# Encoder layer on one core: single-column float32 products in the matmul stream, filter loads moved, first transfers regrouped

## The chip, the cores and the metric

The kernel is one program on one core of a Trainium2 chip. Times are device microseconds (us) of that core. TensorE does the matmuls (PE in the rows; PEld are its weight loads), VectorE (DVE) and ScalarE (ACT) do the elementwise work, GpSimd (POOL) almost nothing, and SyncE (SP) issues most DMA transfers. The engines run side by side and wait for each other by semaphores.

## The reference

The input is x, 256 tokens by 2048 channels, float32. What is computed, cut to its shape:

```
h = rmsnorm(x, norm_mix);  p = h @ w_in            # 2048 -> 4352 columns, shared by three mixers
y_a = pooling over 2/4/8/16 tokens, per-group linear         (512 channels)
y_b = x0 * (conv(x1*v) + d*x1*v), width-3 convolved inputs; conv is a 256-long two-sided
      filter made by a small sine network (two sine layers)  (768 channels)
y_c = u * (128x128 token mixing of layernorm(v)), u, v = gelu (768 channels)
x = x + concat(y_a, y_b, y_c) @ w_out              # 2048 x 2048
h = rmsnorm(x, norm_ffn)
up = dwconv3(h @ ffn_w_up)                         # 2048 -> 11264
x = x + (silu(gate) * val) @ ffn_w_down            # 5632 -> 2048
out = rmsnorm(x, norm_final)
```

## The kernel before

All weights are float32 and are read once from HBM. Every operand of a large product is split into a rounded part (hi) and a rest (lo), and a product is three float32r products: hi with hi, hi with lo, lo with hi. `load_split` (L92) issues the transfer of a chunk on SP, makes hi on ACT (L105) and lo on DVE (L106). Chunks are kept in rings: four raw buffers, three hi and three lo.

The stages, in order of time:

- **v product** (L217, to 42 us): tokens on the partitions, 16 steps over the 2048 input channels, each with 12 products of 384 columns (L233 to L235). Step k needs a 128x768 chunk of weights and a 128x256 piece of x, scaled by the first norm's weight `gmix` (L196, `load_x`). Beside it run the squares for the norm, and the two sine layers that make the filters (`filter_layer1`, L267, and `filter_layer2`, L280: one small float32 product each, L273 and L282, seven DVE operations, one sine on ACT).
- **w_in tiles** (to 226 us): 28 tiles of 128 output channels. A tile is 16 pairs of products (`chunk_products`, L130): one of 512 columns (L137, weights hi, activations hi and lo side by side) and one of 256 (L138, weights lo). Between the chunks of a tile `tick` runs what `at` has put into a slot: the filter's spectrum (`taps_load`, `taps`, `filter_spectrum`), transposes (L408), the forward and inverse transforms (L126 to L128, L459 and L460), pooling (L512) and token mixing (L554). These are the interruptions of the stream of pairs.
- **w_out** (226 to 316 us, 256 pairs on `yT`), **w_up** (to 806 us, 88 tiles, 1408 pairs on `actB`), **w_down** (to 989 us, 528 pairs on `gT`). Shortly after w_up begins come the sums of squares (`sum_cols`, L162: two float32 products of one column) and the broadcast of the norm (`rms_rows`, L180).
- **the last 512 output channels** (L725, `products`), with tokens on the partitions and 512 columns a product, and `finish` (L694): square and sum on ACT, the root, DVE's scaling, the transfers out.

The order on each engine is made by a scheduler from priorities. Loads stand ahead by `tc.high_priority(offset=AHEAD)`. Each engine then works strictly in that order.

A float32 product (not float32r) runs as two records in the trace; so "x4" in a row of L162 is two products.

Of the kernel before, what the change touches and what calls it, by code (L numbers as in the profile page):

```python
# [11 lines left out]
F32 = mybir.dt.float32  # L12
# [25 lines left out]
NWARM = 8  # L38
NAUX = 2

C_GFFN, C_GFIN = 0, 16
# [11 lines left out]
def encoder_layer(ctx, tc, a):  # L53
# [15 lines left out]

    big.tile([P, 24], F32, name="pad_big")  # L70
    xT = big.tile([P, KT, L], F32, tag="xT", name="xT")
    gmix = const.tile([P, KT], F32, name="gmix")
    with tc.high_priority(offset=1000):
        nc.scalar.dma_start(gmix, a["gmix"])
    par = const.tile([P, C_N], F32, name="par")
# [15 lines left out]

    def load_split(src, n, pieces=1, into=None, raw=None, between=None):  # L92
        with tc.high_priority(offset=AHEAD):
            if raw is None:
                raw = wp.tile([P, CW], F32, tag="raw", name="raw", bufs=4)
            hi, lo = into or (wp.tile([P, CW], F32R, tag=t, name=t) for t in ("hi", "lo"))
            for i in range(pieces):
                s = slice(i * n // pieces, (i + 1) * n // pieces)
                (nc.scalar if between and i == 0 else nc.sync).dma_start(raw[:, s], src[:, s])
# [16 lines left out]
    def tick():  # L116
        clock[0] += 1
        for f in slots.pop(clock[0] - 1, []):
            f()

    def split(hi, lo, src):
# [74 lines left out]
    def load_x(ks):  # L196
        nc.sync.dma_start(xT[:, ks[0]:ks[-1] + 1, :], a["xT"][:, ks[0]:ks[-1] + 1, :])
        for k in ks:
# [15 lines left out]
    vtok = p1.tile([P, 2, D_GM], F32, name="vtok")  # L214


    def v_product(then):  # L217
        pv = [[psm.tile([P, 512], F32, tag="mm", name="mm") for _ in range(2)] for _ in range(2)]
        p1.tile([P, 24], F32, name="pad_y")
        head = p1.tile([P, KT // 2, D_GM], F32, tag="yT", name="head")  # L220
        for k in range(KT):
            first = (lambda: load_x(x_steps[0])) if k == 0 else None
            hi, lo = load_split(a["w_v"][k], D_GM, 2 if k == 0 else 1, raw=head[:, k, :] if k < KT // 2 else None,
                                between=first)
            if k + 1 < len(x_steps):
                with tc.high_priority(offset=AHEAD):
                    load_x(x_steps[k + 1])
            for g in range(2):
# [335 lines left out]
    def filters(q, n):  # L564
        taps_load(q)
        for i in range(2):
            at(n + i, lambda i=i: taps(i))
            at(n + 2 + i, lambda i=i: filter_spectrum(q, i))
# [10 lines left out]
    for i in range(2):  # L579
        load_dft(Fh[i].rearrange("p a b -> p (a b)"), a["Fm"][i])  # L580
    filters(0, 2)
    pool_group(0)
# [9 lines left out]
    hyena_out(0, z, Ys)  # L592
    at(0, lambda: filters(1, 1))
    z, zT = hyena_z(1)
# [30 lines left out]
    for c in range(2):  # L625
        for m in range(2):
            chunk_products(head[m], w_out(m), yT, c, KT)
    for m in range(KT):
        ps, sb = (head[m], second_half(head[m])) if m < 2 else proj_tile(w_out(m), yT, KT)
# [11 lines left out]
    p2 = ctx.enter_context(tc.tile_pool(name="p2", bufs=1))  # L641
    p2.tile([P, 32], F32, name="pad_g")
    gT = p2.tile([P, NFF, 2, L], F32R, name="gT")
# [10 lines left out]
    for j in range(NFF):  # L654
        o = []
        for part in range(2):
            m = 2 * j + part
            ps, sb = up[m] if j == 0 else up_tile(m)
            nc.vector.tensor_add(sb, ps[:, :L], sb)
            s = tmp("ev")  # L660
# [33 lines left out]
    def finish(h, ps):  # L694
        t = slice(h * P, (h + 1) * P)
        wide = wp.tile([P, CW], F32, tag="raw", name="raw", bufs=4)
        sq, xt = wide[:, :NL], wide[:, NL:]
        ssq, v, s_, y, w, r = (tmp(f"fin{i}", 1) for i in range(6))
# [25 lines left out]

    def products(h, c, last):  # L725
        hi, lo = chunks[c]
        for i in range(NKC):
# [4 lines left out]
            nc.tensor.matmul(acc[h], lh, lo[:, s], start=False, stop=False)  # L732
            nc.tensor.matmul(acc[h], ll, hi[:, s], start=False, stop=last and i == NKC - 1)  # L733

    for c in range(NC):
        if c >= NKEEP:
            chunks[c] = load_split(a["w_last"][c], CW)
        products(0, c, c == NC - 1)
        if c >= NKEEP:
            products(1, c, False)  # L740
        if c == NKEEP:
            pc = sum_cols(acc3)
            nc.vector.tensor_scalar(rest, pc[:, 0:2], 1.0 / D, EPS_RMS, op0=ALU.mult, op1=ALU.add)
    for c in range(NKEEP):
        products(1, c, c == NKEEP - 1)
        if c == 1:
            finish(0, acc[0])
# [138 lines left out]
```

## Time and profile before

| | us |
|---|---|
| median of 3 runs (1061.39 to 1061.55) | 1061.5 |
| the profiled execution, its own time | 1061.44 |
| its span, first to last instruction | 1059.6 |
| PE busy | 1048.1 (99%) |
| PEld busy | 921.5 (87%) |
| DVE busy | 788.6 (74%) |
| ACT busy | 577.5 (54%) |
| DMA, mean rate | 191 GB/s |

The profiled execution is 0.06 us below the median, and 1.8 us lie around its span. PE's granted clock is half up to 5.4 us from the span's start and full from there to the end of the products. Matmuls overlap in the records (a 512-column product is shown with 391 ns though the next one starts 230 ns later), so their pace is read from start to start and not from their durations.

### The profile page before, as it was taken

How to read it: one execution, taken by the hardware profiler on the slowest of the kernel's cores; microseconds unless marked ns; L12 is line 12 of the kernel's file. 1: busy time of each engine (PE TensorE's matmuls, PEld its weight loads, DVE VectorE, ACT ScalarE, POOL GpSimd, SP SyncE). 2: the span in 40 equal slices, each digit the busy share in tenths (PEclk: the TensorE clock that was granted, in tenths of full speed). 3: DMA queues.
4: the chain of work that ended last, by engine and by line, in shares of the span. 5: the costliest groups of instructions: out<-in, count | busy, mean ns of one | idle time of the engine just before them, and what ended most of it. 6: DMA issues, size and time to landing. Idle time of an engine off the chain costs nothing.

```text
span 1059.6 us, 15714 instructions
## 1 busy us (share of the span) xinstructions
PE 1048.1 (99%) x5956; PEld 921.5 (87%) x5956; DVE 788.6 (74%) x1239; ACT 577.5 (54%) x871; POOL 1.3 (0%) x14
## 2 busy tenths in 40 slices
PE   9999999999999999999999999999999999999997
PEld 8888888888888888888888888888888888888885
DVE  6898998987767878878788888788886555565344
ACT  7765555555556555555555555555555444554332
POOL 0000000000000000000000000000000000000000
PEclk9999999999999999999999999999999999999999
DMA  8866545566555665656556665566565665676462
GB/s 289 270 193 214 173 150 172 206 193 190 187 183 190 194 191 189 194 186 195 183 196 186 191 191 188 192 187 196 184 194 176 196 188 188 229 214 206 143 192 79
DMA packets 62019, 202.83 MB, mean 191 GB/s; under 512 B 7063, under 2 KB 11896, under 8 KB 61816
## 3 DMA queue, kind: packets, MB, share of 16 engines
q1 hardware_dynamic: 61656, 201.64, 59.2%
q8 instruction: 46, 0.75, 0.3%
q10 hardware_dynamic: 288, 0.20, 0.1%
q14 instruction: 29, 0.24, 0.1%
HBM read 199.72 MB, written 2.10 MB: 190 GB/s over the span
## 4 chain that ended last, share of the span: by engine, by line
PE 98%; DVE 1%; DMA 0%; ACT 0%; issue 0%; SPq 0%; DVEq 0%; ACTq 0%
PE mm L137 56%; PE mm L138 29%; PE mm L731 2%; PE mm L733 2%; PE mm L732 2%; PE mm L234 1%; PE mm L233 1%; PE mm L235 1%; PE aux L137 1%; PE aux L127 0%; PE aux L128 0%; DMA xT<-in_xT 0%; DVE lo L106 0%; PE aux L138 0%; PE aux L126 0%; PE aux L459 0%
## 5 line engine op out<-in xcount | busy, mean ns | idle before, releaser
L105 ACT CAST hi<-raw 128x1024 fp32r<-128x1024 f32 (+1 forms) x362 | 373.9, 1033 | 432.5 <-PE mm L137 211.9
L106 DVE TENSOR_TENSOR lo<-raw,hi 128x1024 fp32r<-128x1024 f32 (+1 forms) x362 | 434.8, 1202 | 230.1 <-ACT hi L105 229.3
L137 PE MATMUL mm<-actB,hi 128*128 128x512 f32 x1408 | 488.8, 391 | 0.0
L138 PE MATMUL mm<-actB,lo 128*128 128x256 f32 x1408 | 394.2, 280 | 0.0
L137 PEld LDWEIGHTS mm<-actB,hi 128*128 128x128 f32 x1408 | 263.3, 187 | 58.0 <-DVE actB L635 0.2
L138 PEld LDWEIGHTS mm<-actB,lo 128*128 128x128 f32 x1408 | 266.1, 189 | 0.0
L137 PE MATMUL mm<-gT,hi 128*128 128x512 f32 x528 | 183.1, 391 | 0.0
L137 PE MATMUL mm<-actA,hi 128*128 128x512 f32 x416 | 148.1, 398 | 0.0
L138 PE MATMUL mm<-gT,lo 128*128 128x256 f32 x528 | 147.8, 280 | 0.0
L137 PEld LDWEIGHTS mm<-gT,hi 128*128 128x128 f32 x528 | 98.7, 187 | 21.6
L138 PE MATMUL mm<-actA,lo 128*128 128x256 f32 x416 | 116.6, 280 | 0.0
L138 PEld LDWEIGHTS mm<-gT,lo 128*128 128x128 f32 x528 | 99.8, 189 | 0.0
L137 PEld LDWEIGHTS mm<-actA,hi 128*128 128x128 f32 x416 | 78.1, 188 | 17.3
L137 PE MATMUL mm<-yT,hi 128*128 128x512 f32 x256 | 90.5, 399 | 0.0
L138 PEld LDWEIGHTS mm<-actA,lo 128*128 128x128 f32 x416 | 78.5, 189 | 0.1
L138 PE MATMUL mm<-yT,lo 128*128 128x256 f32 x256 | 71.9, 281 | 0.0
L378 ACT ACTIVATE o<-ev,par 128x256 f32<-128x256 f32 x106 | 63.3, 598 | 8.0 <-DVE ev L373 6.6
L137 PEld LDWEIGHTS mm<-yT,hi 128*128 128x128 f32 x256 | 48.1, 188 | 11.9
L380 DVE SCALAR_TENSOR_TENSOR o<-ev,par,o 128x255 f32<-128x255 f32 x106 | 51.2, 483 | 3.3
L145 ACT COPY sb<-mm 128x256 f32<-128x256 f32 x142 | 51.9, 366 | 0.0
L379 DVE SCALAR_TENSOR_TENSOR o<-ev,par,o 128x255 f32<-128x255 f32 x106 | 50.7, 479 | 0.4 <-ACT o L378 0.4
L138 PEld LDWEIGHTS mm<-yT,lo 128*128 128x128 f32 x256 | 48.4, 189 | 0.0
(208 smaller groups left out, 809.6 us busy)
## 6 DMA issues: line engine op xcount, KB each, us to landing
raw<-in_w_up SPq DMA_DIRECT2D x176, 512.0 KB, 3.5
raw<-in_w_down SPq DMA_DIRECT2D x60, 512.0 KB, 3.7
raw<-in_w_in SPq DMA_DIRECT2D x56, 512.0 KB, 3.5
raw<-in_w_out SPq DMA_DIRECT2D x32, 512.0 KB, 3.5
raw<-in_w_last SPq DMA_DIRECT2D x22, 512.0 KB, 3.5
raw<-in_w_v SPq DMA_DIRECT2D x8, 384.0 KB, 3.5
raw<-in_w_down SPq DMA_DIRECT2D x12, 256.0 KB, 2.6
head<-in_w_v SPq DMA_DIRECT2D x7, 384.0 KB, 6.4
```

The source lines that it names most:

```text
L105: nc.scalar.copy(hi[:, s], raw[:, s])
L106: nc.vector.tensor_sub(lo[:, s], raw[:, s], hi[:, s].bitcast(F32))
L137: nc.tensor.matmul(ps, hi[:, s], act[:, k, :, :], start=k == 0, stop=False)
L138: nc.tensor.matmul(ps[:, :L], lo[:, s], act[:, k, 0, :], start=False, stop=k == nk - 1)
L145: nc.scalar.copy(sb, ps[:, L:])
L233: nc.tensor.matmul(o, actA[:, k, 0, t], hi[:, s], start=k == 0, stop=False)
L378: nc.scalar.activation(o, s, AF.Identity, bias=col(b), scale=col(w1))
L379: nc.vector.scalar_tensor_tensor(o[:, 1:], s[:, :L - 1], col(w0), o[:, 1:], op0=ALU.mult, op1=ALU.add)
L380: nc.vector.scalar_tensor_tensor(o[:, :L - 1], s[:, 1:], col(w2), o[:, :L - 1], op0=ALU.mult, op1=ALU.add)
L731: nc.tensor.matmul(acc[h], lh, hi[:, s], start=False, stop=False)
L732: nc.tensor.matmul(acc[h], lh, lo[:, s], start=False, stop=False)
L733: nc.tensor.matmul(acc[h], ll, hi[:, s], start=False, stop=last and i == NKC - 1)
```

## The change

Five things are changed.

- **Single-column products.** `settle` issues one float32 product of `ones` with one column of `ones` into a spare PSUM bank and keeps it in program order. It is called after the first chunk of w_out, after w_out's first four chunks, and after tile 2 of w_up.
- **Filter loads.** The weights and the decay of the filter taps (`taps_load`), and the transform matrices `Fm`, are loaded inside slots of the w_in tiles instead of ahead of them, and each filter step comes one slot later.
- **First transfers.** `gmix` and the first piece of x come in one transfer on SP. The first chunk of v weights comes in two halves on ACT's queue into a buffer of its own. For the first three steps (`first_loads`) the order on SP, ACT and DVE is the written one.
- **The end.** The last chunk of each token half is done in two halves of 256 columns (12 products instead of 6), and `finish` squares and sums the two halves apart.
- Pads of buffers are changed so that the new buffers fit.

```
+    def settle():
+        tc.keep_in_program_order(nc.tensor.matmul(aux()[:, 0:1], ones, ones[:, 0:1], start=True, stop=True))
...
+    xg = big.tile([P, GX + KT * L], F32, tag="xT", name="xg")
+    xT = xg[:, GX:].rearrange("p (k l) -> p k l", k=KT)
+    gmix = xg[:, GX - KT:GX]
+    w_first = const.tile([P, D_GM], F32, name="w_first")
+    with tc.high_priority(offset=2000):
+        nc.sync.dma_start(xg[:, GX - KT:GX + L], a["first"])
+        nc.scalar.dma_start(w_first[:, :HC], a["w_v"][0][:, :HC])
+    with tc.high_priority(offset=1900):
+        nc.scalar.dma_start(w_first[:, HC:], a["w_v"][0][:, HC:])
...
+    def first_loads(head):
+        parts = []
+        for k in range(NFIRST):
+            if k == 0:
+                parts.append(load_split(None, D_GM, 2, raw=w_first, between=lambda: load_x(x_steps[0])))
+            else:
+                with tc.high_priority(offset=AHEAD):
+                    load_x(x_steps[k])
+                parts.append(load_split(a["w_v"][k], D_GM, raw=head[:, k, :]))
+        return parts
...
     def filters(q, n):
-        taps_load(q)
+        at(0, lambda: taps_load(q))
...
-        load_dft(Fh[i].rearrange("p a b -> p (a b)"), a["Fm"][i])
-    filters(0, 2)
+        at(2, lambda i=i: load_dft(Fh[i].rearrange("p a b -> p (a b)"), a["Fm"][i]))
+    filters(0, 3)
...
             chunk_products(head[m], w_out(m), yT, c, KT)
+            if c == m == 0:
+                settle()
+    settle()
...
             ps, sb = up[m] if j == 0 else up_tile(m)
+            if m == 2:
+                settle()
...
-        nc.scalar.activation(sq, ps, AF.Square, accum_out=ssq)
-        nc.scalar.activation(s_, ssq, AF.Sqrt, scale=1.0 / D, bias=rest[:, h:h + 1])
-        nc.vector.tensor_scalar(v, ssq, 1.0 / D, rest[:, h:h + 1], op0=ALU.mult, op1=ALU.add)
+        nc.scalar.activation(sq[:, :L], ps[:, :L], AF.Square, accum_out=sa)
+        nc.vector.tensor_scalar(more, sa, 1.0 / D, rest[:, h:h + 1], op0=ALU.mult, op1=ALU.add)
+        nc.scalar.activation(sq[:, L:], ps[:, L:], AF.Square, accum_out=ssq)
+        nc.scalar.activation(s_, ssq, AF.Sqrt, scale=1.0 / D, bias=more)
+        nc.vector.tensor_scalar(v, ssq, 1.0 / D, more, op0=ALU.mult, op1=ALU.add)
...
+    def last_products(h, c):
+        hi, lo = chunks[c]
+        for g in range(2):
+            o = acc[h][:, g * L:(g + 1) * L]
+            for i in range(NKC):
+                k = NKC * c + i
+                s = slice(i * NL + g * L, i * NL + (g + 1) * L)
+                lh, ll = (gT[:, k, j, h * P:(h + 1) * P] for j in range(2))
+                nc.tensor.matmul(o, lh, hi[:, s], start=False, stop=False)
+                nc.tensor.matmul(o, lh, lo[:, s], start=False, stop=False)
+                nc.tensor.matmul(o, ll, hi[:, s], start=False, stop=g == 1 and i == NKC - 1)
```

DVE at the program's start, before: the two halves of the first weight chunk (`head`) and the first pieces of activations (`actA`).

```order
L101 CAST hi<-head 128x384
L201 SCALAR_TENSOR_TENSOR actA<-xT,gmix,actA 128x256
L106 TENSOR_TENSOR lo<-head,hi 128x384
L201 SCALAR_TENSOR_TENSOR actA<-xT,gmix,actA 128x256
L101 CAST hi<-head 128x384
L201 SCALAR_TENSOR_TENSOR actA<-xT,gmix,actA 128x256
L106 TENSOR_TENSOR lo<-head,hi 128x384
L106 TENSOR_TENSOR lo<-head,hi 128x768
```

The same place in the changed kernel, where the first chunk is `w_first`.

```order
L111 CAST hi<-w_first 128x384
L216 SCALAR_TENSOR_TENSOR actA<-xg,actA 128x256
L116 TENSOR_TENSOR lo<-w_first,hi 128x384
L111 CAST hi<-w_first 128x384
L116 TENSOR_TENSOR lo<-w_first,hi 128x384
L216 SCALAR_TENSOR_TENSOR actA<-xg,actA 128x256
L116 TENSOR_TENSOR lo<-head,hi 128x768
```

Both halves of the first chunk now come before the second piece of activations; before, two pieces of activations stood between them.

ACT where the v product ends and the w_in tiles begin, before: the last chunk of v weights is the 768 wide CAST, the first chunks of w_in are the 1024 wide ones.

```order
L105 CAST hi<-raw 128x768
L185 ACT_TABLE_LOAD
L185 ACTIVATE rs_s<-rms_v 128x2
L294 CAST F_109<-raw 128x512
L257 ACT_TABLE_LOAD
L257 ACTIVATE w_348<-w_351 64x256
L241 ACT_TABLE_LOAD
L241 ACTIVATE vtok<-mm,rstd_mix 128x384
L105 CAST hi<-raw 128x1024 x3
```

The same place in the changed kernel.

```order
L115 CAST hi<-raw 128x768
L115 CAST hi<-raw 128x1024
L287 ACT_TABLE_LOAD
L287 ACTIVATE w_350<-w_353 64x256
L199 ACT_TABLE_LOAD
L199 ACTIVATE rs_s<-rms_v 128x2
L115 CAST hi<-raw 128x1024 x2
L271 ACT_TABLE_LOAD
L271 ACTIVATE vtok<-mm,rstd_mix 128x384 x3
```

The first chunk of w_in is now cast before the three table loads and their functions, the next two before the gelu (L271), and the cast of `Fm` (F) is gone from here.

On PE nothing of the pairs is moved. The three added products (L133) stand behind 8 pairs of w_out, 24 pairs further on, and 16 pairs behind the broadcast of the norm in w_up, where 1360 pairs on `actB` and 528 on `gT` follow without a break, as in the order before.

ACT at the end, with the semaphores that each instruction waits for, before: the root's argument and the squares of both token halves.

```order
L699 ACTIVATE raw,fin_10374<-mm 128x512 [waits PE_49]
L700 ACT_TABLE_LOAD
L700 ACTIVATE fin_10376<-fin_10374,rest 128x1 [waits Activation_49]
L699 ACTIVATE raw,fin_10414<-mm 128x512 [waits DVE_49,PE_49]
L700 ACTIVATE fin_10416<-fin_10414,rest 128x1 [waits Activation_49]
```

The same in the changed kernel.

```order
L734 ACTIVATE raw,fin_10394<-mm 128x256 [waits PE_49]
L736 ACTIVATE raw,fin_10388<-mm 128x256
L737 ACT_TABLE_LOAD [waits DVE_49]
L737 ACTIVATE fin_10390<-fin_10388,fin_10395 128x1 [waits Activation_49]
L734 ACTIVATE raw,fin_10444<-mm 128x256 [waits PE_49]
L736 ACTIVATE raw,fin_10438<-mm 128x256
L737 ACTIVATE fin_10440<-fin_10438,fin_10445 128x1 [waits DVE_49,Activation_49]
```

There are now two squares for each half of the tokens; the first waits for PE, the second has no wait for PE of its own. The count that the first waits for is the one that PE reaches with the last product of both column halves, since the twelve products raise PE's semaphore only once, at their end.

## Rows read from the trace of the kernel before

**Rows 1.** The page's chain that ended last, by engine.

```profile
PE 98%; DVE 1%; DMA 0%; ACT 0%; issue 0%; SPq 0%; DVEq 0%; ACTq 0%
```

**Rows 2.** Line L137's answer: durations ns min/median/max, first and last start in us.

```profile
L137 PE MATMUL mm<-gT,hi x528: 391/391/391, 805.8 to 988.5; 128*128 128x512 f32 x176
L137 PE MATMUL mm<-actA,hi x416: 388/395/578, 58.0 to 224.8; 128*128 128x512 f32 x139
L137 PE MATMUL mm<-yT,hi x256: 395/398/447, 226.0 to 316.2; 128*128 128x512 f32 x128
```

**Rows 3.** Timeline of PE at w_up's start: start us, us, instruction.

```profile
316.54 0.40 PE L137 MATMUL mm<-actB,hi 128*128 128x512 f32 x1
...
321.84 0.40 PE L137 MATMUL mm<-actB,hi 128*128 128x512 f32 x1
...
322.72 0.50 PE L162 MATMUL aux<-ones,acc 128*128 128x1 f32 x4
323.09 0.48 PE L137 MATMUL mm<-actB,hi 128*128 128x512 f32 x1
...
323.52 0.40 PE L137 MATMUL mm<-actB,hi 128*128 128x512 f32 x1
...
328.03 0.39 PE L137 MATMUL mm<-actB,hi 128*128 128x512 f32 x1
```

**Rows 4.** Timeline of PE around a transpose among the w_in tiles.

```profile
165.86 0.40 PE L137 MATMUL mm<-actA,hi 128*128 128x512 f32 x1
...
176.26 0.40 PE L137 MATMUL mm<-actA,hi 128*128 128x512 f32 x1
...
176.61 0.39 PE L408 MATMUL aux<-ident,z 128*128 128x128 f32 x2
...
177.20 0.40 PE L137 MATMUL mm<-actA,hi 128*128 128x512 f32 x1
...
184.97 0.40 PE L137 MATMUL mm<-actA,hi 128*128 128x512 f32 x1
```

**Rows 5.** Timeline of the first 9 us; in brackets the idle time before.

```profile
0.73 0.40 ACTq L74 DMA_DIRECT2D gmix<-in_gmix  x1
...
4.38 0.36 DVE L101 CAST hi<-head 128x384 fp32r<-128x384 f32 x1 [3.38 <-DMA head<-in_w_v]
...
5.17 0.72 PE L233 MATMUL mm<-hi,actA 128*128 128x384 f32 x2 [0.34 <-DVE actA L201]
...
7.00 0.48 DVE L201 SCALAR_TENSOR_TENSOR actA<-xT,gmix,actA 128x256 fp32r<-128x256 f32 x1 [0.73 <-ACT actA L200]
7.39 0.83 ACT L105 CAST hi<-head 128x768 fp32r<-128x768 f32 x1 [0.42 <-DMA head<-in_w_v]
7.40 0.55 DVE L106 TENSOR_TENSOR lo<-head,hi 128x384 fp32r<-128x384 f32 x1
...
8.01 0.44 PE L234 MATMUL mm<-lo,actA 128*128 128x384 f32 x1 [1.00 <-DVE lo L106]
```

**Rows 6.** Timeline of PE, then of ACT, where w_in begins.

```profile
42.07 0.34 PE L235 MATMUL mm<-hi,actA 128*128 128x384 f32 x1
43.12 0.50 PE L137 MATMUL aux<-actA,hi 128*128 128x512 f32 x1 [0.71 <-ACT hi L105]
43.46 0.59 PE L180 MATMUL aux<-rms_dg,ones 128*128 128x256 f32 x2
44.75 0.39 PE L138 MATMUL aux<-actA,lo 128*128 128x256 f32 x1 [0.69 <-DVE lo L106]
...
42.04 2.93 ACT L105 CAST hi<-raw 128x1024 fp32r<-128x1024 f32 x3
```

**Rows 7.** Timeline of ACT at the end, and the squares of 256 columns (L617).

```profile
1051.51 0.60 ACT L699 ACTIVATE raw<-mm 128x512 f32<-128x512 f32 x1 [4.78 <-PE mm L733]
1052.23 0.29 ACT L700 ACTIVATE fin<-fin,rest 128x1 f32<-128x1 f32 x1
...
L617 ACT ACTIVATE sq<-xT x26: 401/404/419, 241.7 to 992.1; 128x256 f32<-128x256 f32 x26
```

More of the change, by code (lines that the diff above doesn't have):

```diff
@@ L39 @@
 NAUX = 2
+NFIRST = 3
+GX = 64
 C_GFFN, C_GFIN = 0, 16
@@ L67, in aux @@
         return psa.tile([P, 512], F32, tag="aux", name="aux")
[L70 to L74, printed above, removed]
+    big.tile([P, 40], F32, name="pad_big")
+    xg = big.tile([P, GX + KT * L], F32, tag="xT", name="xg")
[7 more added lines that the diff above has]
+        nc.scalar.dma_start(w_first[:, HC:], a["w_v"][0][:, HC:])
     par = const.tile([P, C_N], F32, name="par")
@@ L98, in load_split @@
                 s = slice(i * n // pieces, (i + 1) * n // pieces)
-                (nc.scalar if between and i == 0 else nc.sync).dma_start(raw[:, s], src[:, s])
+                if src is not None:
+                    nc.sync.dma_start(raw[:, s], src[:, s])
                 if pieces > 1:
@@ L196, in load_x @@
     def load_x(ks):
-        nc.sync.dma_start(xT[:, ks[0]:ks[-1] + 1, :], a["xT"][:, ks[0]:ks[-1] + 1, :])
+        if ks[0]:
+            nc.sync.dma_start(xT[:, ks[0]:ks[-1] + 1, :], a["xT"][:, ks[0]:ks[-1] + 1, :])
         for k in ks:
@@ L214, in encoder_layer @@
     vtok = p1.tile([P, 2, D_GM], F32, name="vtok")
+    def first_loads(head):
[8 more added lines that the diff above has]
+        return parts
     def v_product(then):
         pv = [[psm.tile([P, 512], F32, tag="mm", name="mm") for _ in range(2)] for _ in range(2)]
-        p1.tile([P, 24], F32, name="pad_y")
+        p1.tile([P, 56], F32, name="pad_y")
         head = p1.tile([P, KT // 2, D_GM], F32, tag="yT", name="head")
         for k in range(KT):
[L222 to L227, printed above, removed]
+            if k == 0:
+                with tc.manual_schedule(engines={mybir.EngineType.SP, mybir.EngineType.Activation, mybir.EngineType.DVE}):
+                    parts = first_loads(head)
+            if k < NFIRST:
+                hi, lo = parts[k]
+            else:
+                if k < len(x_steps):
+                    with tc.high_priority(offset=AHEAD):
+                        load_x(x_steps[k])
+                hi, lo = load_split(a["w_v"][k], D_GM, raw=head[:, k, :] if k < KT // 2 else None)
             for g in range(2):
@@ L592, in encoder_layer @@
     hyena_out(0, z, Ys)
-    at(0, lambda: filters(1, 1))
+    filters(1, 2)
     z, zT = hyena_z(1)
@@ L641, in encoder_layer @@
     p2 = ctx.enter_context(tc.tile_pool(name="p2", bufs=1))
-    p2.tile([P, 32], F32, name="pad_g")
+    p2.tile([P, 64], F32, name="pad_g")
     gT = p2.tile([P, NFF, 2, L], F32R, name="gT")
@@ L697, in finish @@
         sq, xt = wide[:, :NL], wide[:, NL:]
-        ssq, v, s_, y, w, r = (tmp(f"fin{i}", 1) for i in range(6))
-        nc.scalar.activation(sq, ps, AF.Square, accum_out=ssq)
-        nc.scalar.activation(s_, ssq, AF.Sqrt, scale=1.0 / D, bias=rest[:, h:h + 1])
-        nc.vector.tensor_scalar(v, ssq, 1.0 / D, rest[:, h:h + 1], op0=ALU.mult, op1=ALU.add)
+        ssq, v, s_, y, w, r, sa, more = (tmp(f"fin{i}", 1) for i in range(8))
+        nc.scalar.activation(sq[:, :L], ps[:, :L], AF.Square, accum_out=sa)
[3 more added lines that the diff above has]
+        nc.vector.tensor_scalar(v, ssq, 1.0 / D, more, op0=ALU.mult, op1=ALU.add)
         nc.vector.reciprocal(y, s_)
@@ L723, in encoder_layer, with products @@
                              stop=False)
-    def products(h, c, last):
+    def last_products(h, c):
[9 more added lines that the diff above has]
+                nc.tensor.matmul(o, ll, hi[:, s], start=False, stop=g == 1 and i == NKC - 1)
+    def products(h, c):
         hi, lo = chunks[c]
@@ L732, in products @@
             nc.tensor.matmul(acc[h], lh, lo[:, s], start=False, stop=False)
-            nc.tensor.matmul(acc[h], ll, hi[:, s], start=False, stop=last and i == NKC - 1)
+            nc.tensor.matmul(acc[h], ll, hi[:, s], start=False, stop=False)
     for c in range(NC):
@@ L737, in encoder_layer @@
             chunks[c] = load_split(a["w_last"][c], CW)
-        products(0, c, c == NC - 1)
+        (last_products if c == NC - 1 else products)(0, c)
         if c >= NKEEP:
-            products(1, c, False)
+            products(1, c)
         if c == NKEEP:
@@ L744, in encoder_layer @@
     for c in range(NKEEP):
-        products(1, c, c == NKEEP - 1)
+        (last_products if c == NKEEP - 1 else products)(1, c)
         if c == 1:
@@ L852 @@
         "xT": i["x"][0].T.reshape(KT, P, L).transpose(1, 0, 2),
-        "gmix": _cols(i["norm_mix"][0]),
+        "first": np.concatenate([_cols(i["norm_mix"][0]), i["x"][0].T[:P]], axis=1),
         "par": par,
```

## The prediction

> **What bounds the kernel now.** I read the page's chain first: 98% of it is PE [rows 1], so only three things can move the time by more than tenths: PE's pace, its waits, and the tail behind its last product. Idle time of ACT and DVE counts only where PE waits for it.
>
> For the pace I took line L137 by stage, start to start. In w_down, 528 pairs start between 805.8 and 988.5 us, 182.7/527 = 0.3467 us a pair; in w_out, 256 start between 226.0 and 316.2, 90.2/255 = 0.3537 [rows 2]. The shapes are the same. It could be the tile that is read, so I looked where one tile runs at both paces, at w_up's start [rows 3]. The 16 starts from 316.54 to 321.84 give 5.30/15 = 0.3533; then come two one-column float32 products (L162); and the 14 starts from 323.52 to 328.03 give 4.51/13 = 0.3469. The tile `actB` is the same before and after. So the pace is a condition of PE that lasts until something interrupts the pairs, and an interruption can change it. The slow pace costs 6.6 ns a pair.
>
> An interruption can also go the other way. Among the w_in tiles, 31 starts from 165.86 to 176.26 give 0.3467; after a transpose, also float32, the 23 from 177.20 to 184.97 give 7.77/22 = 0.353 [rows 4]. That is the danger of this change.
>
> For PE's waits I read the timelines of the two places where PE stands: the start [rows 5] and the beginning of w_in [rows 6]. The tail is in [rows 7].
>
> **The change part by part.** The sum is made against the profiled execution, 1061.44 us (span 1059.6, 1.8 around it); the median of the runs is 0.06 above.
>
> *w_out's two products.* w_out enters at the slow pace and keeps it up to L162 in w_up: 256 pairs and 17 of w_up (316.54 to 322.26). The first added product stands behind 8 of them. If the pace is fast from there, (273 − 8) × 6.6 ns = **−1.75 us**. The nearest row is L162 itself, the only one-column product among pairs: it went from slow to fast. The ends: nothing, or all of it.
>
> *Cost of a one-column product.* L162's two stand from 322.72 to 323.09, 0.37 us in which a pair would have begun, and the pair behind takes 323.09 to 323.52, 0.43 instead of 0.347 [rows 3]: 0.45 for two, 0.23 each. Three: **+0.69 us**. The bank that each needs was last used over 130 products earlier for the first two, so I add no wait.
>
> Here the Trainium skill speaks against the change: "TensorE: Matmul & The Clock Gate", section "Wait — 56ns, not 53.3ns?", gives a product its columns by 2.4 GHz and some 2.5 ns, with no memory of what came before. By that rule a pair takes 325 ns always, the added products could only cost, and the sum below would lose its 1.75 us. The trace does not agree: 346.7 and 353 ns for the same pair.
>
> *w_up's product.* In the kernel before, w_up and w_down run at the fast pace throughout, so nothing is to be gained; the product's price is in the 0.69. What it puts at risk is below.
>
> *The start.* PE's first product is at 5.17, behind a first half of weights that was cast at 4.38, on arrival; its transfer was issued on ACT's queue behind `gmix`, which holds that queue for 0.40 us. PE then sat idle 1.0 us until 8.01 for the lo of the second half, at 7.40 on DVE, and DVE had idled 0.73 before 7.00 for the activation of a later piece of x [rows 5]. In the new order no later piece of x stands ahead of that lo. With the first half 0.4 earlier, DVE's five steps (0.36 + 0.48 + 0.55 + 0.36 + 0.55 = 2.3 us) end at 3.95 + 2.3 = 6.3 instead of 7.95, if the second half lands by 5.4. Then the next thing is late: step 1's lo. Its chunk landed at 7.39, and is now issued ahead of one piece of x; taken as landing at 6.7, ACT's 0.83 and DVE's 0.96 (twice the 384 columns' 0.55, less its fixed part) end at about 8.5. There PE has the 12 products of step 0 and 3 of step 1 behind it. Before, at 8.5, it was at the 11th (8 done at 8.01, and some 0.2 each from there). Four to five products of 0.173 us (half a pair's columns) are 0.8, and the 0.4 at the front brings later steps forward too: I take **−1.0 us**. Ends: −0.4 (the issue alone) and −1.4 (the 1.0 of idle time and the 0.4).
>
> *The filter loads.* Where w_in begins, PE's L235 at 42.07 is followed by L137 only at 43.12, waiting for ACT's hi, 1.05 us instead of 0.17; and behind L180 at 43.46 the next pair starts at 44.75, waiting for DVE's lo, 1.29 instead of about 0.3 (two records of 256 columns, a third of a pair each): 0.88 + 1.0 = 1.9 us of standing. ACT's first cast of w_in came at 42.04 [rows 6], behind three table loads, a cast of `Fm` and a gelu. In the new order that cast stands ahead of all these, and its transfer is no longer behind the two of `Fm` and their raw buffers. Also L180 comes a tile later. What is late next: PE waits in order for the second sine layer's input at L312 and for the norm's diagonal at L194, both now behind ACT's later table loads; by the durations here they come about 1 us before PE asks. I take **−1.8 us**; ends 0 (the stall moves) and −1.9. The steps of the filter come one slot (half a tile, 8 pairs or 2.8 us) later, and nothing on PE asked for them that closely.
>
> *The w_in tiles.* Their interruptions move, so their pace may too. `actA`'s median of 395 ns lies between the slow 398 and the fast 391 [rows 2], about half and half; 448 pairs × 6.6 ns = 3.0 us lies between the extremes, so 0, with ±1.5 for the range.
>
> *The end.* The second square waits for nothing of PE, and the first for the last of the twelve products: the halves do not overlap with PE. One pass of 512 columns is 1052.23 − 1051.51 = 0.72 us; one of 256 is shorter by 0.598 − 0.404 = 0.19 [rows 7], 0.53; two are 1.06, **+0.34 us** (−0.2 if the halves did overlap, one shorter pass behind the last product). Twelve products of 256 columns stream as many columns as six of 512, so 0 there, with up to 0.1 for the more weight loads. The same for the first token half is covered by PE's products on the second.
>
> Sum: −1.75 + 0.69 − 1.0 − 1.8 + 0 + 0.34 = −3.5 us, **1057.9 us**.
>
> **Rivals.**
> - *w_out stays or falls back slow* (its second product does what the transpose did [rows 4], or the first does nothing). For it: both directions are in the trace. Against: L162. Then the 1.75 is gone: 1059.6. Chance 0.15.
> - *The stall at w_in's beginning moves* to L312, L194 or the lo of the first chunk. For it: DVE's and ACT's orders there are dense, with four table loads. Against: the cast that PE waited for is now first. Without the 1.8: 1059.7. Chance 0.10.
> - *Slower: the product in w_up leaves PE slow.* It stands where before 1904 pairs at the fast pace followed L180; now 1360 + 528 = 1888 pairs follow it. If it goes the transpose's way, 1888 × 6.6 ns = 12.5 us are lost: 1070.4. It decides from 3.5/0.0066 = 530 slow pairs on, under a third of them. For it: [rows 4]. Against: L162 ended fast, and no product of that form ended slow. Chance 0.12.
> - The forecast: 0.63.
>
> **How the numbers follow.** A measurement tells this kernel from no change at about 0.2%, 2.1 us. Forecast's own range: 1055.6 to 1059.6 (ends of the start, of w_in's pace and of the tail, not all at once). The first two rivals, and both together at 1061.4, belong to the range; the slow w_up stays out with its 0.12. Range 1055.0 to 1061.0. Faster (under 1059.3): 0.58 of the forecast's 0.63 and about half of the two at 1059.6 and 1059.7, 0.71. Slower: 0.12 and 0.01 of pile-ups, 0.13. The same: 0.16.
>
> **What would show it.** Pairs on `yT` from the second chunk on, and on `actB` and `gT`, at 0.3467 us a start: right; at 0.353: that step is wrong. The sum is refuted as a whole if w_up runs at 0.353. PE's first lo product of the second half without a second's idle before it; no step over 0.5 us between the last L235 and the fourth pair of w_in; two ACT squares behind the last product, 0.3 us longer together. If PE still stands 1 us for hi or lo where w_in begins, the filter step is wrong.

## The result and the profile after

The changed kernel takes **1071.47 us** (median of 4 runs, 1071.15 to 1071.91) against 1061.53 us before: ratio 1.0093, 95% interval 1.0076 to 1.0111. It is slower by 10 us; the forecast was 1057.9. What happened is the third rival, priced at 1070.4: the product in w_up leaves PE slow. The profiled execution took 1071.91 us, its span is 1070.0 (before 1059.6). Of the 103 runs of the kernel before in the experiments 7, on two of the four chips, took 1073.6 to 1075.6 us and the rest 1060.6 to 1062.9; no trace of such a run was taken, and since they shift some of the ratios below (to 0.9999 where the medians are 1064.15 and 1061.84), differences here are of medians.

The page's chain by engine, where [rows 1] had 98% for PE:

```profile
PE 96%; DVE 1%; DMA 1%; ACT 1%; issue 0%; SPq 0%; DVEq 0%; ACTq 0%
```

PE still bounds the kernel. The answer on the line of the pairs (L151, L137 before), with durations in ns as min/median/max and the first and last start:

```profile
L151 PE MATMUL mm<-actB,hi x1408: 392/398/577, 313.7 to 811.8; 128*128 128x512 f32 x176
L151 PE MATMUL mm<-gT,hi x528: 395/398/403, 812.2 to 998.4; 128*128 128x512 f32 x176
...
L151 PE MATMUL mm<-yT,hi x256: 392/395/478, 224.2 to 313.3; 128*128 128x512 f32 x128
```

Against [rows 2], gT has gone from 391 to 398 and yT from 398 to 395. On gT 186.2/527 = 0.3533 us a pair, where it was 0.3467: the slow pace, in all of w_down. Where it begins shows the timeline of PE in w_up, around the third added product (L133; the lo products, L152, are left out):

```profile
330.39 0.40 PE L151 MATMUL mm<-actB,hi 128*128 128x512 f32 x1
...
330.74 0.39 PE L151 MATMUL mm<-actB,hi 128*128 128x512 f32 x1
...
331.09 0.40 PE L151 MATMUL mm<-actB,hi 128*128 128x512 f32 x1
...
331.44 0.28 PE L133 MATMUL aux<-ones 128*128 128x1 f32 x2
331.58 0.48 PE L151 MATMUL mm<-actB,hi 128*128 128x512 f32 x1
...
332.01 0.40 PE L151 MATMUL mm<-actB,hi 128*128 128x512 f32 x1
...
332.36 0.40 PE L151 MATMUL mm<-actB,hi 128*128 128x512 f32 x1
...
332.71 0.40 PE L151 MATMUL mm<-actB,hi 128*128 128x512 f32 x1
```

Ahead of the product 0.39 and 0.40 alternate; behind it every hi takes 0.40, and so it stays for 1888 pairs. The starts in ns give three patterns of steps from pair to pair, and they are the key to all that follows:

- *even*: 347, 346, 347 (mean 346.7); w_up and w_down of the kernel before;
- *in turn*: 350, 343, 350, 343 (also 346.7); behind [rows 3]'s L162, and here ahead of the third product;
- *slow*: 349, 350, 361 in a round of three (353.3).

In w_out, PE around the first and the second added product:

```profile
226.75 0.40 PE L151 MATMUL mm<-yT,hi 128*128 128x512 f32 x1
...
227.10 0.28 PE L133 MATMUL aux<-ones 128*128 128x1 f32 x2
227.24 0.48 PE L151 MATMUL mm<-yT,hi 128*128 128x512 f32 x1
...
227.67 0.40 PE L151 MATMUL mm<-yT,hi 128*128 128x512 f32 x1
...
228.03 0.40 PE L151 MATMUL mm<-yT,hi 128*128 128x512 f32 x1
...
235.81 0.28 PE L133 MATMUL aux<-ones 128*128 128x1 f32 x2
235.95 0.47 PE L151 MATMUL mm<-yT,hi 128*128 128x512 f32 x1
...
236.38 0.40 PE L151 MATMUL mm<-yT,hi 128*128 128x512 f32 x1
...
236.73 0.39 PE L151 MATMUL mm<-yT,hi 128*128 128x512 f32 x1
```

The first leaves the pairs slow (0.36 from 227.67 to 228.03), the second makes them fast. Each takes 0.14 us and makes the pair behind it 0.43: 0.22 together, as forecast (0.23).

The start and the beginning of w_in, PE's timeline:

```profile
4.54 0.79 PE L263 MATMUL mm<-hi,actA 128*128 128x384 f32 x2
5.53 0.45 PE L264 MATMUL mm<-lo,actA 128*128 128x384 f32 x1 [0.20 <-DVE lo L116]
...
38.30 0.34 PE L265 MATMUL mm<-hi,actA 128*128 128x384 f32 x1
38.98 0.70 PE L312 MATMUL aux<-w,fw 64*128 64x256 f32 x2 [0.34 <-ACT w L287]
...
41.80 0.39 PE L151 MATMUL aux<-actA,hi 128*128 128x512 f32 x1
...
53.33 0.34 PE L140 MATMUL aux<-w3p,f 128*128 128x384 f32 x1
53.81 0.44 PE L141 MATMUL aux<-w3p,f 128*128 128x384 f32 x1
...
62.38 0.44 PE L141 MATMUL aux<-k,F 128*128 128x384 f32 x1 [0.45 <-DVE k L137]
```

The second of idle time of [rows 5] is gone, and so are both stalls of [rows 6]. But PE waits in three other places: at the second sine layer (38.30 to 38.98, 0.50 beyond a product's step of 0.17, where the kernel before waits 0.20), between the taps' products (0.48 instead of 0.17 at 53.33), and in the first spectrum at 62.38. The first of these has to do with an order that section "The change" does not show: the sine layer's product (L312) stands 12 products of 384 columns ahead of the end of the v product, where the kernel before has 7 behind it, so PE asks for its input five products, 0.87 us, sooner.

At the end, PE's last product and ACT's two squares:

```profile
1061.23 0.28 PE L773 MATMUL mm<-kept,gT 128*128 128x256 f32 x1
1061.55 0.38 ACT L734 ACTIVATE raw<-mm 128x256 f32<-128x256 f32 x1 [4.72 <-PE mm L773]
...
1061.92 0.38 ACT L736 ACTIVATE raw<-mm 128x256 f32<-128x256 f32 x1
...
1062.42 0.29 ACT L737 ACTIVATE fin<-fin,fin 128x1 f32<-128x1 f32 x1
```

From the first square to the root 0.87 us, 0.72 in [rows 7]. The path by stages, the first start of each on PE:

| | before | after | difference |
|---|---|---|---|
| first product | 5.17 | 4.54 | -0.63 |
| 101st product of 384 columns | 24.12 | 23.36 | -0.76 |
| first pair of w_in | 43.12 | 41.80 | -1.32 |
| first pair of w_out | 226.04 | 224.23 | -1.81 |
| first pair of w_up | 316.54 | 313.69 | -2.85 |
| first pair of w_down | 805.83 | 812.19 | +6.36 |
| last product | 1051.08 | 1061.23 | +10.15 |
| span | 1059.6 | 1070.0 | +10.4 |

1360 slow pairs behind the product in w_up are 9.07 us and the 528 of w_down 3.52: 12.6, which turn a lead of 2.85 us into a lag of 10. The end costs more than ACT's 0.15: from the last pair of w_down to the root it takes 64.04 us against 63.71, 0.3 us.

### The profile page after: what moved, and what is told of

Same layout as the page of the kernel before. It is cut to its first block, busy times and chain, and to the rows that moved or that the text cites. A ratio compares the mean times of both kernels' runs of the same rounds, so it can differ in the third digit from the quotient of the medians.

```text
span 1070.0 us, 15760 instructions
## 1 busy us (share of the span) xinstructions
PE 1059.6 (99%) x5974; PEld 923.6 (86%) x5974; DVE 788.9 (74%) x1241; ACT 578.6 (54%) x876; POOL 1.3 (0%) x14
## 4 chain that ended last, share of the span: by engine, by line
PE 96%; DVE 1%; DMA 1%; ACT 1%; issue 0%; SPq 0%; DVEq 0%; ACTq 0%
PE mm L151 57%; PE mm L152 29%; PE mm L781 2%; PE mm L783 2%; PE mm L782 2%; PE mm L264 1%; PE mm L263 1%; PE mm L265 1%; DVE lo L116 1%; DMA head<-in_w_v 1%; PE aux L141 0%; PE aux L142 0%; DMA raw<-in_w_in 0%; PE aux L489 0%; PE aux L140 0%
## 5 line engine op out<-in xcount | busy, mean ns | idle before, releaser
L151 PE MATMUL mm<-actB,hi 128*128 128x512 f32 x1408 | 497.9, 399 | 0.0
L152 PE MATMUL mm<-actB,lo 128*128 128x256 f32 x1408 | 395.3, 281 | 0.0
L151 PEld LDWEIGHTS mm<-actB,hi 128*128 128x128 f32 x1408 | 264.5, 188 | 66.0 <-DVE actB L668 0.3
L152 PEld LDWEIGHTS mm<-actB,lo 128*128 128x128 f32 x1408 | 265.9, 189 | 0.0
L151 PE MATMUL mm<-gT,hi 128*128 128x512 f32 x528 | 186.6, 399 | 0.0
L152 PE MATMUL mm<-gT,lo 128*128 128x256 f32 x528 | 148.3, 281 | 0.0
L151 PE MATMUL mm<-actA,hi 128*128 128x512 f32 x416 | 148.0, 398 | 0.0
L151 PEld LDWEIGHTS mm<-gT,hi 128*128 128x128 f32 x528 | 99.2, 188 | 24.8
L152 PE MATMUL mm<-actA,lo 128*128 128x256 f32 x416 | 116.2, 279 | 0.0
L152 PEld LDWEIGHTS mm<-gT,lo 128*128 128x128 f32 x528 | 99.7, 189 | 0.0
L151 PEld LDWEIGHTS mm<-actA,hi 128*128 128x128 f32 x416 | 78.1, 188 | 16.9
L151 PE MATMUL mm<-yT,hi 128*128 128x512 f32 x256 | 89.3, 395 | 0.0
L152 PEld LDWEIGHTS mm<-actA,lo 128*128 128x128 f32 x416 | 78.5, 189 | 0.1
L152 PE MATMUL mm<-yT,lo 128*128 128x256 f32 x256 | 71.0, 278 | 0.0
L151 PEld LDWEIGHTS mm<-yT,hi 128*128 128x128 f32 x256 | 48.0, 188 | 11.1
L152 PEld LDWEIGHTS mm<-yT,lo 128*128 128x128 f32 x256 | 48.1, 188 | 0.0
```

Source lines behind the costliest of these rows:

```text
L151: nc.tensor.matmul(ps, hi[:, s], act[:, k, :, :], start=k == 0, stop=False)
L152: nc.tensor.matmul(ps[:, :L], lo[:, s], act[:, k, 0, :], start=False, stop=k == nk - 1)
```

## The experiments

Each kernel is the changed one with the edit shown, unless told otherwise. Times are medians; the ratio is against the kernel before on the same chip (its medians there were 1061.4 to 1061.8, so two times from different chips can differ by some tenths for that alone).

**Without the third product.**

```
-            if m == 2:
-                settle()
```

> The changed kernel without its third added product (the one in w_up behind tile 1). Theory A, a single one-column product turned the pace of w_up and w_down from 346.7 to 353.3 ns a pair: w_up and w_down then run at 346.7 a pair throughout, the answers on actB and gT read a mean of about 391 and 391 again, and the time is 1071.5 - 1888 x 6.67 ns (12.6) - 0.2 = 1058.7 us. Rival R, w_up's pace comes from something else of the change (the place of gT and actB in memory behind the wider pads, or L194's different phase): the pairs stay at 353.3 and the time is 1071.2.

1058.91 us, ratio 0.9976 (0.9967 to 0.9985). The line's answer on gT:

```profile
L151 PE MATMUL mm<-gT,hi x528: 392/394/395, 804.5 to 987.2; 128*128 128x512 f32 x176
```

182.7/527 = 0.3467 us a pair, at the same address of gT. The rival falls: one product of one column costs 12.6 us, and the rest of the change is a gain of 2.5 to 3.

**Two in its place.**

```
             if m == 2:
                 settle()
+                settle()
```

> The changed kernel with two one-column products, back to back, where it has its third. Theory A1, each product steps the pace on, and it was an odd one that left it slow: two in a row leave it as it was, as the pair of L176 did a few tiles earlier; w_up at 346.7, time 1071.5 - 12.6 + 0.25 = 1059.1. Theory A2, any interruption at this place of w_up ends slow: 353.3 a pair and 1071.7.

1059.40 us, ratio 0.9971 (0.9948 to 0.9994). Pairs in turn ahead of the two and in turn behind them. So neither the place nor the interruption as such is bad; one product there, with the pairs in turn, is.

**None of the three.** The two calls in w_out and the one in w_up are left out.

> The changed kernel without all three added products; the start, the filter loads and the end stay as changed. Theory A: w_out runs at 353.3 a pair up to L176 in w_up and everything behind it at 346.7, so against no_third the time gains 1.6 us of slow pairs and loses 0.5 of products: 1059.8, which is 1.7 below the kernel before and is what the start, the junction and the end are worth together. Rival R: w_up stays at 353.3, 1072.3. Were the start and the junction worth nothing, 1061.5 to 1061.9.

1060.24 us, ratio 0.9986 (0.9976 to 0.9996). w_out is slow up to L176, and w_up is fast. The two products of w_out are thus worth 1060.24 - 1058.91 = 1.3 us; from the first pair of w_out to the first of w_down the two traces differ by 1.10 (579.77 and 578.67).

**The kernel before with the third product alone.**

```
             ps, sb = up[m] if j == 0 else up_tile(m)
+            if m == 2:
+                settle()
```

> The kernel before with one one-column product added where the changed kernel has its third, and nothing else. Theory A: a single product there leaves w_up and w_down at 353.3 a pair: 1061.5 + 12.6 + 0.2 = 1074.3. Theory A3, it depends on which of the two fast patterns the pairs are in (steps of 343 and 350 ns in turn in the changed kernel, 346 and 347 in the kernel before), and from the even steps one product leads to a fast one: 1061.7.

1062.18 us, ratio 1.0006 (0.9973 to 1.0040): A is wrong, A3 right. In the trace the 16 pairs ahead are even and the 1888 behind are even. The same instruction at the same place cost nothing beyond its own time here. One of the ten runs took 1075.06 us; it has no trace.

**The changed kernel once more**, nothing edited.

> The changed kernel once more, with nothing edited, for how its runs spread: the kernel before had two of 31 runs at 1073.7 us, 12 above the rest, which is the size of a slow w_up. Theory A, the third product always meets the pairs in the same pattern and always leaves them slow: every run within 1071 to 1073. Theory C, the pattern is drawn anew in each run: part of the runs at about 1059, part at 1071.5.

1071.75 us (1070.97 to 1073.44, 10 runs), ratio 1.0074 (1.0041 to 1.0108). None of the ten is near 1059: here the outcome is not drawn anew.

**The third product without the two in w_out.**

> The changed kernel without its two products in w_out, with the third in w_up kept. Without all three, the pairs that reach the place of the third run in steps of 343 and 350 ns in turn, as in the changed kernel. Theory A, what decides is that pattern: one product there leaves 353.3 a pair, 1060.2 + 12.6 + 0.2 = 1073.0. Theory P, what decides is how many one-column products came before (an odd or an even number): then w_up stays at 346.7 and the time is 1060.5.

Neither: of ten runs six took 1072.6 to 1073.3 us and four 1059.9 to 1061.0 (median 1072.72, ratio 1.0036, 0.9989 to 1.0083). In the trace, one of the six, the pairs ahead ran in turn. The number of products before doesn't decide, since it was the same in all ten.

**One tile later.**

```
-            if m == 2:
+            if m == 3:
```

> The changed kernel with its third product one tile (16 pairs) later in w_up. Theory A, the pattern that it meets is the same (343 and 350 in turn) and decides: 1872 pairs at 353.3, 1071.4. Rival, it is the spot, 16 pairs behind the broadcast of the norm, that is bad: 1059.1.

1071.85 us, ratio 1.0081 (1.0051 to 1.0112): slow from the product on, behind 32 pairs in turn. Not the spot.

**The old end, no third product.** L734 to L738 and the last chunk's products as in the kernel before.

> The changed kernel without the third product and with the end of the kernel before (one square over 512 columns, products of 512 columns in the last chunk). By the profile the two squares take 0.33 us longer behind the last product than the one: 1058.9 - 0.3 = 1058.6 with w_up at 346.7 a pair. Rival, the two halves do overlap with something and the change of the end is worth a little: 1059.1.

1064.15 us, ratio 0.9999 (0.9968 to 1.0031): both theories miss by 5 us, and it taught something else. The old norm needs two scratch tiles fewer, which moved yT and gT from a multiple of 256 bytes to 128 beyond one. Line L151 on gT:

```profile
L151 PE MATMUL mm<-gT,hi x528: 387/396/400, 805.3 to 990.4; 128*128 128x512 f32 x176
```

185.03/527 = 0.3511 us a pair, with the third product gone; actB, which had not moved, ran at 0.3467 behind L176. I had varied two things at once.

**The old end with yT and gT in their place.**

```
-    p1.tile([P, 56], F32, name="pad_y")
+    p1.tile([P, 88], F32, name="pad_y")
-    p2.tile([P, 64], F32, name="pad_g")
+    p2.tile([P, 96], F32, name="pad_g")
```

> The run with the old end again (no third product), with 128 bytes of padding more ahead of yT and gT. Without them two tiles fewer in the last norm had moved both from a multiple of 256 bytes to 128 beyond one, and its pairs on yT and gT took 351.1 ns and its last products 231 instead of 227. Theory Q, the place of the tile sets that: pairs at 346.7, products at 227, and what is left is the end's own 0.33: 1058.9 - 0.3 = 1058.6 us. Theory S, it was the wide products or the single square: still 1064.

1058.71 us, ratio 0.9970 (0.9959 to 0.9982), and on gT:

```profile
L151 PE MATMUL mm<-gT,hi x528: 392/394/395, 802.6 to 985.3; 128*128 128x512 f32 x176
```

0.3467 again: the place of the tiles was worth those 5 us. Between the two traces 4.6 of them are seen: 0.9 us in w_out, 2.3 in w_down (528 x 4.4 ns) and 1.4 in the last stage, whose 512-column products take 232 ns a start instead of 227. In w_out and w_down the moved tile is the operand that streams through PE; in the last stage gT is the operand that is loaded as weights, and what streams there had not moved. The Trainium skill's "SBUF — State Buffer", section "Operand start alignment", asks only that an operand starts at a multiple of its element's size, and says of its own runs that they timed nothing; both places are legal by it, and here they differ by 4.4 ns a pair. The new end costs 0.2 us by the medians (1058.91 against 1058.71, on two chips, with intervals that overlap), and by the traces 0.31: from the last pair of w_down to the root 64.00 us in the run without the third product, 63.70 here.

**The first filter's steps a tile later.** As the run before, and

```
-    filters(0, 3)
+    filters(0, 5)
```

> As the run with the old end in the old place of yT and gT, and the taps and spectra of the first filter a whole tile later (two slots). In the changed kernel PE waits 0.3 us for the first filter's taps at 53.3 us and 0.3 to 0.9 for its spectrum's input at 61.6 to 62.7; in the kernel before it waited for neither. Theory F, ACT and DVE reach them late because the loads and casts of the tables stand behind the first w_in casts now, and a tile of slack hides it: 0.6 to 1.2 us less, 1057.7. Rival, they wait again where they are now: 1058.6.

1058.92 us, ratio 0.9974 (0.9964 to 0.9984): no gain. The taps' products come five us later (58.71 instead of 53.33), and PE waits among them all the same:

```profile
64.39 0.45 PE L140 MATMUL aux<-w3p,f 128*128 128x384 f32 x1 [0.73 <-DVE e L356]
```

PE's last group of taps starts when DVE has multiplied an earlier one with the decay (L356, at 63.79), which stands behind other work on DVE; a tile of slack for the loads does not touch that. Theory F had half of the reason: in the trace without the third product the first taps did wait for ACT's cast of their weights (0.32 us at 53.91), and that wait is gone here, but this one has come in its place.

**The old filter loads**, without the three products.

```
-        at(0, lambda: taps_load(q))
+        taps_load(q)
-        at(2, lambda i=i: load_dft(..., a["Fm"][i]))
-    filters(0, 3)
+        load_dft(..., a["Fm"][i])
+    filters(0, 2)
-    filters(1, 2)
+    at(0, lambda: filters(1, 1))
```

> The changed kernel without its three products and with the filter loads where the kernel before has them; start and end stay changed. My prediction's term: they were worth 1.8 us, so 1060.2 + 1.8 = 1062.0. Theory F, most of that came back as waits at the second sine layer (0.5), the taps (0.3) and the spectrum (0.3 to 0.8), so they were worth 0.1 to 0.7: 1060.3 to 1060.9.

1062.11 us, ratio 1.0001 (0.9992 to 1.0010): 1.9 us above the run without the three products, as my prediction's term for the loads (1.8) has it. But six of these ten runs show a mean granted clock of 0.996, which no other run of any kernel has, and took 1061.96 to 1062.99 us; the four at 0.997 and 0.998 took 1060.72 to 1061.57, median 1061.3. By these four the old loads cost 1.1 us. So the loads are worth 1.1 to 1.9, and this kernel, with the changed start and the changed end, lies between 0.4 us above and 0.4 below the kernel before; with the end's 0.3 taken off, the start is worth 0 to 0.7. PE's timeline (of a run of 1061.57, clock 0.997):

```profile
38.21 0.34 PE L265 MATMUL mm<-hi,actA 128*128 128x384 f32 x1
39.67 0.70 PE L312 MATMUL aux<-w,fw 64*128 64x256 f32 x2 [1.12 <-ACT w L287]
...
42.65 0.49 PE L151 MATMUL aux<-actA,hi 128*128 128x512 f32 x1
43.90 0.39 PE L152 MATMUL aux<-actA,lo 128*128 128x256 f32 x1 [0.77 <-DVE lo L116]
```

PE is early (0.85 us at the 101st product) and waits 1.3 us for the second sine layer's input, at which PE had stood 0.2 in the trace of before. ACT's sine did come earlier, at 39.20 instead of 39.83, but PE asks sooner by its lead and by the five products in the order. Of its lead on the kernel before 0.47 us are left at the first pair of w_in, 0.37 at that of w_out and 0.29 at that of w_down, and the end takes as much.

**A fourth product, one tile behind the third.**

```
-            if m == 2:
+            if m in (2, 3):
```

> The changed kernel with a fourth one-column product, one tile (16 pairs) behind the third. Theory A, a product from the slow pattern leads to a fast one, as the second in w_out did: 16 pairs at 353.3, then 1872 at 346.7: 1071.5 - 12.5 + 0.2 = 1059.2. Rival, one from the slow pattern leaves it slow, as the first in w_out did: 1071.9.

1072.50 us, ratio 1.0100 (1.0085 to 1.0116): slow behind it too. A falls: a product from the slow pattern may leave it (the second of w_out) or not (the first, and this one).

What the cases have in common I then looked for in the steps. A product stands in for the next pair's start, so it breaks off the pattern at one of its steps. Counted so, the products that ended fast had come where a step of 349 was due (the first after a 361), and the others at 350 or 361; from pairs in turn both had come at a 350. That rule was tested next.

**One pair later.** The third product behind 17 pairs instead of 16, where a 343 is due.

```
+            pairs[0] += 1
+            if pairs[0] in marks:    # marks = {49}, counted from w_up's first pair
+                settle()
```

> The changed kernel with its third product one pair later: behind 17 pairs since the norm's broadcast instead of 16. The pairs run in steps of 350 and 343 ns in turn; at 16, and at 32 pairs in another run, the step broken off was one of 350, and what followed was slow both times. Theory P, the step that is broken off decides: at 17 it is one of 343, and the pairs behind it are fast: 1059.1 us. Rival, from that pattern every single product ends slow: 1071.5.

1059.40 us, ratio 0.9979 (0.9970 to 0.9988). PE around the product:

```profile
331.25 0.40 PE L153 MATMUL mm<-actB,hi 128*128 128x512 f32 x1
...
331.60 0.39 PE L153 MATMUL mm<-actB,hi 128*128 128x512 f32 x1
...
331.94 0.28 PE L133 MATMUL aux<-ones 128*128 128x1 f32 x2
...
332.52 0.40 PE L153 MATMUL mm<-actB,hi 128*128 128x512 f32 x1
...
332.87 0.39 PE L153 MATMUL mm<-actB,hi 128*128 128x512 f32 x1
```

0.39 and 0.40 still alternate behind it. One pair's difference in place is worth 12 us.

**One product in w_out, behind 7 pairs.** On the version with the old end in the old place; marks = {7} in w_out.

> The best version so far (old end in the old place, no product in w_up) with one product in w_out instead of two, behind 7 pairs. The slow pairs run in steps of 349, 350 and 361 in turn. The product that made them fast (behind 24 pairs of its kind) came in the first step after one of 361; those that left them slow came in the second (behind 8, the first in w_out) and in the one of 361 itself (the fourth in w_up). Theory P: behind 7 it is the first after one of 361, so the pairs are fast from there; one product (0.23) and 25 slow pairs (0.17) less than 1058.7: 1058.3. Rival, w_out stays slow up to its sums of squares: 1058.7 + 1.75 - 0.2 = 1060.2.

1058.52 us, ratio 0.9972 (0.9962 to 0.9982): the lowest median of all versions. The pairs are in turn from the product on, as the rule has it. The gain over two products is within the uncertainty of the times; from the first pair of w_out to the first of w_down the traces differ by 0.39 us (578.28 and 578.67; 0.40 expected).

**78 places in one run.** Products in w_up behind 16, 17, 18, 15, 19 and 20 pairs, over and over.

> The changed kernel with 78 one-column products in w_up instead of one, 15 to 20 pairs apart, to see after each which pattern follows. Its time is no comparison: 1058.9 + 78 x 0.23 = 1076.8 if all pairs were fast, up to 9 more if all were slow. Theory P: the pattern ahead and the step in it that is broken off give the pattern behind; the same two always lead to the same, and slow patterns follow from about a third to a half of the places. Rival, chance: the same two lead now to a fast pattern and now to a slow one.

1080.67 us. What followed, from the starts in the trace:

| pairs ahead | step broken off | products | pairs behind |
|---|---|---|---|
| in turn | 343 | 26 | fast, 26 of 26 |
| in turn | 350 | 13 | slow, 13 of 13 |
| slow | 349, first after 361 | 13 | fast, 13 of 13 |
| slow | 350, second after 361 | 13 | slow, 13 of 13 |
| slow | 361 | 13 | slow, 13 of 13 |

No exception: for single products it is a rule of the place in the pattern, not chance. (Fast here was always in turn.) The 78 places are not 78 different cases: the distances repeat, and from the second place on the patterns go round with them in the same six cases. That it is the step and not the number of pairs ahead rests on the runs together: 15, 17 and 19 pairs ahead of a 343, 16, 20 and 32 ahead of a 350, and 7, 18 and 24 ahead of the 349.

**Three more runs of the third product without those of w_out.**

> The kernel without the products in w_out and with the third in w_up, looked at again: of its ten runs six took 1072.6 to 1073.3 us and four 1059.9 to 1061.0, and the one with a trace was one of the six. Theory P: where the time is about 1060, the pairs ahead of the product ran in even steps (346 and 347), which a product left fast in the kernel before; where it is about 1073, in steps of 343 and 350. Rival, chance: the same steps ahead of it and both outcomes.

> As the run before it in this list, a third look: about 1060 us with even steps of 346 and 347 ahead of the product, or about 1073 with steps of 343 and 350 (theory P); the same steps with both outcomes (chance).

> As the two runs before it in this list, a fourth look: about 1060 us with even steps of 346 and 347 ahead of the product, or about 1073 with steps of 343 and 350 (theory P); the same steps with both outcomes (chance).

1059.86, 1060.51 and 1060.45 us. The first of them ahead of the product:

```profile
331.45 0.39 PE L151 MATMUL mm<-actB,hi 128*128 128x512 f32 x1
331.80 0.39 PE L151 MATMUL mm<-actB,hi 128*128 128x512 f32 x1
332.14 0.28 PE L133 MATMUL aux<-ones 128*128 128x1 f32 x2
```

and the trace of a run of 1073:

```profile
332.10 0.39 PE L151 MATMUL mm<-actB,hi 128*128 128x512 f32 x1
332.44 0.40 PE L151 MATMUL mm<-actB,hi 128*128 128x512 f32 x1
332.79 0.28 PE L133 MATMUL aux<-ones 128*128 128x1 f32 x2
```

In all three traces of about 1060 us the pairs are even ahead of it, in that of 1073 in turn, as theory P of these three has it (the step, not the odd or even number that P stood for in the first run of this kernel). It goes back to L176: it left the pairs at 353.3 ns in the three and even in the other; L194 turned the first into even steps and the second into steps in turn. Why L176, two products, does now this and now that is open; the step that it breaks off does not tell. In seven traces it met slow pairs at the same place in their round, and its first product began 451 ns after the last pair (in turn behind it: the third product in the kernel before), 453 to 454 (slow: these three and the old loads) or 459 to 460 (even: the run of 1073 and the one without products). The outcomes sort by that time; no run was made to test it.

## Why the prediction was wrong

**The step that failed** is that of *w_up's product*. I put the risk that it leaves PE slow at 0.12 with "L162 ended fast, and no product of that form ended slow". But L162 is two products back to back, and the trace held no single one among pairs: two in a row at the fatal place ended fast as well. The row that I called the nearest was of another form. I had also priced the product by the kernel before, where one at this place does no harm, as the pairs come to it even; in the changed kernel they come in turn. The price of the rival was right: 12.5 us forecast, 12.6 by the slow pairs of the trace (12.8 by the medians 1071.75 and 1058.91, with the product's own 0.2). What decided was not whether a product can leave PE slow but which step it breaks off, and for that the two-decimal starts of [rows 3] are too coarse; both patterns of the fast pace look like 0.35 there.

**w_out's two products**: -1.75 and 0.46 of cost forecast, -1.29 together; -1.33 by the medians, -1.10 by the traces. The size is right and the way to it was luck in part: L162 spoke no more for these two than for the third. The first did nothing and the second did it, 24 pairs later (0.16 us). Against the rule of the Trainium skill that the prediction weighed ("TensorE: Matmul & The Clock Gate", section "Wait — 56ns, not 53.3ns?": columns by the clock and a fixed extra, nothing of what ran before) the runs stand firmer than the trace did: the same pair takes 346.7 or 353.3 ns after one and the same product.

**The start**, -1.0: three quarters of it reached on PE (-0.63 at the first product, -0.76 at the 101st), and worth 0 to 0.7 us in the time with the old loads, so how much of it is kept is open; their trace has 0.37 left at w_out.

**The filter loads**, -1.8: 1.1 to 1.9 between the two kernels that differ in it, and not for its reason alone, since part of it is the wait at L312. That the sine layer's input would "come about 1 us before PE asks" was wrong: PE waited 0.50 us there, and 1.3 without the new loads. Start and loads together are worth 1.7 us (1061.68 - 1060.24, and the 0.3 of the end), not 2.8. The waits at L312, the taps and the spectrum belong to what was given back; how the missing 1.1 splits between the two terms is not shown.

**The w_in tiles**: no term, and 0.49 us less in the table above, from the waits and the patterns together; the two were not taken apart.

**The end**, +0.34: right in its sum, +0.31 by the traces, but only half of it is ACT's (+0.15). The two squares start 0.37 us apart, not 0.53, since the second begins while the first one's accumulator is read (the trace has the read from 1061.83 to 1062.02, and the second square from 1061.92). The other 0.16 are on PE's side, between the last pair of w_down and the first square, where I had 0 to 0.1.

Without the third product the forecast would have been 1057.7, and 1058.9 was measured; the missing 1.2 lies in the start and the loads together.

## What to carry to other kernels

A number for an operation holds for its form and its place: two in a row is not one, and a row that ended well is no evidence for another position. Where a long stretch of equal work follows a tiny edit, look at the series of its steps in ns before and behind, and weigh the rival by what it would cost, not by how rare it looks. When an edit changes scratch tiles, compare the addresses of the big ones too, or the experiment varies two things.

## What the runs showed of the hardware

A pair of float32 products (512 and 256 columns, a new weight load each) runs at 346.7 or 353.3 ns a pair until something interrupts it; the granted clock is full from 10 us on at the latest to the end of the products in every trace. A one-column product leaves it at either pace, by the step that it breaks off (table above, 78 of 78). With the streaming tile at 128 bytes beyond a multiple of 256 the pair takes 351.1 ns, and with the tile of the weights there the 512-column products of the last stage take 232 instead of 227. What in the chip keeps the place in the pattern is open.
